# A gated-DeltaNet decoder layer: the token projections as blocks of 512 channels, with q, k, v and the attention queries transposed afterwards

## The chip, the core and the metric

The kernel runs on one core of one Trainium2 chip, in float32. The metric is the device time of one launch in microseconds, as the median of several runs. Everything happens in that one launch, with the inputs laid out beforehand by tiles in device memory.

## The reference, cut to what matters

One layer (DEPTH is 1) works on 256 tokens and 256 memory tokens of 2048 channels. Three things are multiplied onto each other at the end: a gated DeltaNet over 24 heads, a four-head cross-attention into the memory, and a SiLU gate over all 4096 inner channels.

```python
mem_n = rms_norm(mem, mem_norm_g)
h     = rms_norm(x, norm_g)
proj  = h @ dn_w_in                  # (256, 11312): q 1536 | k 1536 | v 3072 | a, b 48 | xq 1024 | z 4096
qkv   = silu(causal_depthwise_conv(proj[:, :6144], conv_w))      # 4 taps along the tokens
# per head: q, k l2-normed; g = -exp(a_log) * softplus(a + dt); beta = sigmoid(b)
o     = rms_norm(gated_delta_rule(q, k, v, g, beta), out_g)      # 24 heads of 128, state 128 x 128
xa    = softmax(rms_norm(xq) @ rms_norm(mem_n @ w_k).T / 16) @ (mem_n @ w_v)
y     = concat(o, xa) * silu(z)
out   = x + y @ w_out                # (256, 4096) @ (4096, 2048)
```

The convolution runs along the tokens for each channel by itself, which is why the kernel wants q, k and v with the channels on the partitions and the tokens along the row.

## The kernel before, in words

**Numbers.** Every large product is made exact by splitting each factor into a rounded part (`hi`, type float32r, made by a cast) and its remainder (`lo`, by a subtraction); three products hi·hi, hi·lo and lo·hi are summed in PSUM.

**The weight stream.** `PLAN` (line 51) lists 273 weight loads of 512 KB in the order in which TensorE wants them. `wraw` (line 271) issues a load on SyncE's queue into one of five raw buffers `st`; `wnext` (line 310) casts it on ScalarE to `hi` (line 326) and subtracts it on VectorE to `lo` (line 330), into one of four buffers `wt`; `wload` (line 335) keeps two loads ahead. Loads of kind Z fetch, for each partition, four pieces of 1 KB from four 128-channel weight tiles; all others are one piece of 4 KB per partition.

**Two forms of a projection.** `proj_a` (line 346) makes 128 channels at a time with channels on the partitions: the weights stand still and the tokens move. It takes 16 steps over the 2048 input channels, and each step is a pair of matmuls, one with 512 columns (hi and lo of the 256 tokens beside each other) and one with 256 (the weights' `lo` against the tokens' `hi`, added into the second half). The two halves of its bank are added afterwards in `halves` (line 375): a copy of 128x512 out of PSUM on ScalarE, an addition of 128x256 on VectorE. The 56 tiles of xq (8), k (12), q (12) and v (24) are made like this. `proj_b` (line 385) makes 512 channels at a time with tokens on the partitions, in two banks (r = 0 and 1, 128 tokens each); the tokens stand still and the weights move, with three matmuls of 512 columns per token half and step, 96 in all. The gate (z, `PLAN` kind "Z"), the memory's keys and values ("K", "V") and the output projection ("o") are made like this. In the first and the last load of a block, `proj_b` does all of r = 0 ahead of r = 1, so the r = 0 bank is done six matmuls before the block's end.

**What follows a projection.** A q, k or v tile goes through `conv` (line 813): one scaled copy on ScalarE, three multiply-adds on VectorE, one SiLU on ScalarE, all with the channels on the partitions. A k tile then feeds `gram` (line 846), whose results feed `inverse` (line 893: a loop of 31 small VectorE steps for six pairs of heads, twice) and `merge` (line 956: many small matmuls). `delta` (line 1108) runs the recurrence for one pair of heads: it begins when `Y` of the pair, its v tiles and the delta of the pair before are there. xq tiles go to `xq_done` (line 730) and `attend` (line 755); the latter takes the sum of squares of the query by four small matmuls into a bank of tag "tr" named `xss`. `split_y` (line 1057) transposes each finished 256-channel group of y (`pyT`) and splits it into hi and lo for the output projection, which takes the groups in the order 12 to 15 (attention), 0 to 11.

**PSUM.** The eight banks are dealt out by tag (line 168): `pa` 2, `m` 2, `tr` 1, `A` 2, `B` 1. Successive blocks of `proj_b` alternate between the two `A` and the two `pa` banks; `delta` also takes its banks `pU` and `pO` from `A`.

**The order of the work.** One Python loop (line 1269) writes out TensorE's projections in the order of `PLAN`. Everything else is a generator on a heap; after each group of matmuls `step_side` (line 214) lets those go on whose time has come by a modelled clock `now`, which adds a modelled cost per instruction (lines 122 to 133 and 198 to 208). `pe_soon` (line 228) postpones a process's next matmuls until its inputs should be there, plus 0.7 us; `calm` (line 240) keeps the VectorE's modelled queue under 1.6 us. The instructions of one engine run in the order in which they are queued. So a matmul whose input is late holds up every matmul behind it.

Of the kernel before, what the change touches and what calls it, by code (L numbers as in the profile page):

```python
# [44 lines left out]
LATE_DECAY = ("q", 3)  # L45
SPLIT = ("q", 9)
# [6 lines left out]


def _tiles(*ts):
    for t in ts:
        PLAN.extend([t, t])


for _t in range(8):  # L60
    _tiles(("x", _t))

for _t in range(6):
    _tiles(("k", _t))
    PLAN.extend([("Z", 6 + _t // 3)] * (3, 3, 2, 4, 4, 0)[_t])
for _t in range(3):
    PLAN.extend([("Z", _t)] * 8)
for _t in range(NPAIR):
    _tiles(("q", _t), ("v", 2 * _t), ("v", 2 * _t + 1))
    if _t < 2:  # L70
        _tiles(*[("k", _k) for _k in ((6, 7, 8), (9, 10, 11))[_t]])
    if _t in (1, 4, 7):
        PLAN.extend([("Z", 3 + _t // 3)] * 8)
# [4 lines left out]
STREAM = [_k for _k in PLAN if _k[0] != "Z"] + [("z", _t) for _t in range(32) for _ in range(2)]  # L78
N_PLAIN = len(PLAN) - 64
# [3 lines left out]
def hybrid_kernel(ctx: ExitStack, tc: tile.TileContext, x, xT, memT, W, prm_d, cst_d, out):  # L83
# [66 lines left out]
    s2p = ctx.enter_context(tc.tile_pool(name="s2p", bufs=60))  # L150
# [7 lines left out]
    def SM(name, shape, bufs=3, dt=F32):  # L158
        n = 1
        for d in shape:  # L160
            n *= d
        if n > 128:
            return smp.tile([128] + list(shape), dt, name=name, tag="s1k", bufs=10)
# [34 lines left out]
    def mm(o_, lhsT, rhs, start, stop):  # L198
# [3 lines left out]
        else:  # L202
            now[0] += max(0.092, n / 2400.0 + 0.017)
# [62 lines left out]
    wpos, plain, zpos = [0], [0], {}  # L266
# [4 lines left out]
    def wraw():  # L271
# [5 lines left out]
        if kind == "Z":  # L277

            s4 = zpos.get(t, 0)
            zpos[t] = s4 + 1  # L280
            u = N_PLAIN + 8 * t
# [3 lines left out]
        else:  # L285
            data = W[plain[0]]
# [23 lines left out]
    def wnext():  # L310
# [5 lines left out]
        if kind == "Z":  # L316
            hi, lo = [h.rearrange("p (k t c) -> p k t c", k=2, t=4) for h in (hi, lo)]
# [28 lines left out]
    def proj_a(done, tag="pa"):  # L346


        hold(lambda: spare(tag))
        pt = PS(tag, "pa")  # L350
        for kt in range(NKT):
            if kt % 8 == 0:
                wt = wload()
            hold(lambda: hs[kt] is not None)
            c = slice(kt % 8 * 128, (kt % 8 + 1) * 128)
            mm(pt, wt[:, 0, c], hs[kt].rearrange("p a t -> p (a t)"), start=(kt == 0), stop=False)
            mm(pt[:, 256:512], wt[:, 1, c], hs[kt][:, 0, :], start=False, stop=(kt == NKT - 1))
            if kt == NKT - 1:
                done(pt)
            yield kt % 8 == 7  # L360

# [23 lines left out]
    def proj_b(steps, act, tag, done, before=None):  # L385

        hold(lambda: spare(tag))
        pts = [PS(tag, "pb0"), None]
        n = len(steps)
        for s in range(0, n, 2):  # L390
# [8 lines left out]
            for i, (r, k2) in enumerate(rk):  # L399
                if pts[r] is None:  # L400
                    hold(lambda: spare(tag))
                    pts[r] = PS(tag, "pb1")
# [323 lines left out]

    xag = [None] * 4
    xq = [None] * 8

    def xq_done(t):  # L730
        def done(pt):
            hd, dt = t // 2, t % 2
            if dt == 0:
                xq[hd] = (S2("xqh", [2, 256], F32R), S2("xql", [2, 256], F32R), S2("xsq", [2, 256]))

            def go():
                yield 0.2
                qh, ql, sq = xq[hd]
                qf = yield from halves(pt)
                se.copy(qh[:, dt, :], qf)  # L740
                se.activation(sq[:, dt, :], qf, AF.Square)
                yield
                ve.tensor_tensor(out=ql[:, dt, :], in0=qf, in1=qh[:, dt, :], op=ALU.subtract)
                if dt == 1:
                    yield from attend(hd, qh, ql, sq)
# [9 lines left out]
    def attend(hd, qh, ql, sq):  # L755
        ve.tensor_tensor(out=sq[:, 0, :], in0=sq[:, 0, :], in1=sq[:, 1, :], op=ALU.add)
        yield from pe_soon()
# [10 lines left out]
        rq = SM("rq", [10], 2)  # L768
        ve.tensor_scalar(out=rq[:, 0:2], in0=pss[:, 0:2], scalar1=1.0 / 256, scalar2=EPS, op0=ALU.mult, op1=ALU.add)
        give(pss, ve.end)  # L770
        ve.tensor_reduce(out=rq[:, 4:6], in_=sc.rearrange("p (r m) -> p r m", r=2), axis=AX.X, op=ALU.max)
        yield
        rsqrt(rq[:, 2:4], rq[:, 0:2], 2)
# [39 lines left out]
    def conv(pt, ct, dst, name):  # L813
        acc = SM("acc", [256])
        w0 = P_CW + 4 * ct
        yield 0.2
        raw = yield from halves(pt)
        se.activation(acc, raw, AF.Copy, scale=prm[:, w0 + 3 : w0 + 4])
        yield
        for j in (1, 2, 3):  # L820
            ve.scalar_tensor_tensor(out=acc[:, j:256], in0=raw[:, 0 : 256 - j], scalar=prm[:, w0 + 3 - j : w0 + 4 - j],
                                    in1=acc[:, j:256], op0=ALU.mult, op1=ALU.add)
        yield
# [533 lines left out]
```

## Time and profile before

| | |
|---|---|
| median of 3 runs (lowest to highest) | 869.36 us (869.18 to 870.35) |
| the profiled execution's own time | 867.82 us |
| its span in the trace | 866.0 us |
| TensorE matmuls busy | 860.1 us (99%), 5092 instructions |
| TensorE weight loads busy | 729.3 us (84%) |
| VectorE busy | 638.8 us (74%) |
| ScalarE busy | 536.2 us (62%) |
| GpSimd busy | 39.5 us (5%) |
| DMA | 165.89 MB, mean 192 GB/s |

The span is the part of the execution that the trace covers; the execution's own time is 1.8 us longer, and the median of the timed runs is 1.5 us above that of the profiled execution. "PE" is the TensorE matmul, "PEld" its weight load, which overlaps the matmul before it; DVE is VectorE, ACT ScalarE, POOL GpSimd, SP SyncE. In the chain of waits the time is followed back from the last instruction to whatever released it. Its pieces have a start in us, a length in us, and what ran, with the number of instructions.

### The profile page before, as it was taken

To read this page: it belongs to the slowest core of one execution; us is meant where nothing else is said; L and a number is where in the kernel's file an instruction comes from. 1 tells how busy PE (TensorE), PEld (TensorE's weight loads), DVE (VectorE), ACT (ScalarE), POOL (GpSimd) and SP (SyncE) were. 2 spreads that over 40 slices of the span, in tenths; PEclk is the share of its full clock that TensorE was granted. 3 is DMA by queue.
4 is the path that set the end of the run, shared out by engine and by line. 5 is a ranking of instruction groups with operands and counts; after the bars stand their busy time and mean duration, and the time that the engine had idled before them with its cause. 6 is when DMAs were issued, how large, how long until landed. Compare 5 with 4: busy or idle time off the path is not lost.

```text
span 866.0 us, 13821 instructions
## 1 busy us (share of the span) xinstructions
PE 860.1 (99%) x5092; PEld 729.3 (84%) x5092; DVE 638.8 (74%) x1277; ACT 536.2 (62%) x904; POOL 39.5 (5%) x47
## 2 busy tenths in 40 slices
PE   9999999999999999999999999999999999999998
PEld 6888889888888888888888888878888888888886
DVE  7778898678786999588799898736888755454542
ACT  7655656678776665665578877756777654333331
POOL 1000000000010000001000010000000000000000
PEclk9999999999999999999999999999999999999999
DMA  9865554467878857555756546644344547766660
GB/s 353 312 208 183 171 173 145 135 200 223 266 223 232 256 195 189 193 167 185 209 191 201 190 146 205 182 138 146 122 147 146 170 155 231 235 205 206 204 199 25
DMA packets 97612, 165.89 MB, mean 192 GB/s; under 512 B 23280, under 2 KB 62984, under 8 KB 97544
## 3 DMA queue, kind: packets, MB, share of 16 engines
q1 hardware_dynamic: 97112, 164.72, 59.9%
q8 instruction: 40, 0.66, 0.3%
q10 hardware_dynamic: 432, 0.28, 0.1%
q14 instruction: 28, 0.23, 0.1%
HBM read 158.14 MB, written 6.84 MB: 191 GB/s over the span
## 4 chain that ended last, share of the span: by engine, by line
PE 99%; DMA 1%; DVE 0%; ACTq 0%; issue 0%; DVEq 0%
PE pb L96 51%; PE pa L96 37%; PE pO L96 2%; PE pm L96 2%; PE pkq L96 1%; PE pU L96 1%; PE pyT L96 1%; PE xsc L96 1%; PE xo L96 1%; PE pkk L96 1%; PE pvt L96 1%; DMA mst<-memT_d 1%; PE pqs L96 0%; PE pab L96 0%; PE xpT L96 0%; PE pk L96 0%
## 5 line engine op out<-in xcount | busy, mean ns | idle before, releaser
L330 DVE TENSOR_TENSOR wt<-st,wt 128x1024 fp32r<-128x1024 f32 (+1 forms) x274 | 333.5, 1218 | 143.8 <-ACT wt L326 140.1
L326 ACT CAST wt<-st 128x1024 fp32r<-128x1024 f32 (+1 forms) x274 | 286.3, 1047 | 173.1 <-PE pb L96 127.6
L96 PE MATMUL pa<-hkt,wt 128*128 128x512 f32 (+1 forms) x1792 | 334.6, 341 | 0.0
L96 PEld LDWEIGHTS pa<-hkt,wt 128*128 128x128 f32 x1792 | 274.3, 188 | 38.0 <-ACT zs L113 0.3
L96 PE MATMUL pb<-wt,hkt 128*128 128x512 f32 x768 | 182.2, 393 | 0.0
L96 PEld LDWEIGHTS pb<-wt,hkt 128*128 128x128 f32 x768 | 141.8, 188 | 28.9
L96 PE MATMUL pb<-wt,yhi 128*128 128x512 f32 x512 | 158.7, 391 | 0.0
L96 PEld LDWEIGHTS pb<-wt,yhi 128*128 128x128 f32 x512 | 95.3, 188 | 19.3
L96 PE MATMUL pb<-wt,ylo 128*128 128x512 f32 x256 | 99.7, 390 | 0.0
L96 PE MATMUL pb<-wt,mkt 128*128 128x512 f32 x384 | 91.3, 397 | 0.8 <-DVE mkt L113 0.5
L96 PEld LDWEIGHTS pb<-wt,mkt 128*128 128x128 f32 x384 | 72.7, 191 | 17.9 <-DVE wt L330 1.5
L113 DVE SCALAR_TENSOR_TENSOR acc<-raw,prm,acc 128x255 f32<-128x255 f32 x144 | 68.7, 478 | 6.9 <-ACT acc L113 5.8
L113 ACT COPY raw<-pa 128x512 f32<-128x512 f32 x56 | 32.8, 586 | 45.6 <-PE pa L96 45.5
L96 PEld LDWEIGHTS pb<-wt,ylo 128*128 128x128 f32 x256 | 48.1, 188 | 10.1
L113 ACT ACT_TABLE_LOAD x33 | 42.3, 1283 | 3.2 <-DVE acc L113 2.0
L113 DVE TENSOR_TENSOR raw<-raw 128x256 f32<-128x256 f32 x57 | 23.9, 419 | 14.6 <-ACT raw L113 14.3
L113 DVE TENSOR_TENSOR inT<-inXT,inN 96x1 f32<-96x1 f32 (+22 forms) x92 | 29.8, 342 | 1.0 <-PE pO L96 0.3
L113 DVE TENSOR_REDUCE inXT<-inT 96x1 f32<-96x1 f32 (+22 forms) x92 | 28.8, 337 | 0.6
L113 POOL TENSOR_TENSOR e<-e,mhalf 128x4 f32<-128x4 f32 x12 | 15.4, 1283 | 297.4 <-DVE e L113 277.0
L113 ACT ACTIVATE acc<-raw,prm 128x256 f32<-128x256 f32 x48 | 24.5, 510 | 4.9 <-DVE raw L113 4.9
L113 DVE TENSOR_SCALAR dec<-erow,gcc 128x128 f32<-128x128 f32 x96 | 23.8, 279 | 4.5 <-DMA erow<-dgc 4.5
L113 ACT ACTIVATE dec<-dec 128x512 f32<-128x512 f32 x24 | 15.2, 631 | 12.8 <-DVE dec L113 12.6
(197 smaller groups left out, 666.5 us busy)
## 6 DMA issues: line engine op xcount, KB each, us to landing
st<-W_d SPq DMA_DIRECT2D x272, 512.0 KB, 4.0
erow<-dgc SPq DMA_DIRECT2D x24, 256.0 KB, 4.8
dN<-dec SPq DMA_DIRECT2D x12, 256.0 KB, 3.6
xraw<-xT_d SPq DMA_DIRECT2D x8, 256.0 KB, 6.0
res<-x_d SPq DMA_DIRECT2D x8, 256.0 KB, 5.2
mst<-memT_d SPq DMA_DIRECT2D x7, 256.0 KB, 6.6
out_dram<-res SPq DMA_DIRECT2D x7, 256.0 KB, 5.0
inN<-dN SPq DMA_DIRECT2D x4, 192.0 KB, 4.3
```

Of the source, the lines that this page charges most:

```text
L96: return lambda *a, **k: pin(getattr(self.eng, op)(*a, **k))
L113: return pin(getattr(self.eng, op)(*a, **k))
L326: pin(se.eng.copy(hi[:, w] if parts > 1 else hi, st[:, w] if parts > 1 else src))
L330: pin(ve.eng.tensor_tensor(out=lo[:, w] if parts > 1 else lo, in0=st[:, w] if parts > 1 else src, in1=hi[:, w] if parts > 1 else hi, op=AL ...
```

## The change

All projections of tokens take the form of `proj_b`. The weights in memory stay in tiles of 128 channels; every load of x, k, q, v and z now gathers four pieces of 1 KB per partition, as the Z loads did. `proj_a`, `halves` for these tiles, `conv` and `xq_done` go. After a block of k, q or v, `tiles_done` copies the two banks to SBUF (two copies of 128x512 on ScalarE), transposes them on TensorE in two groups of four 128x128 pieces into a bank of tag "m" (two channel tiles per bank), and does the convolution of each tile with its input read from that bank. `x_done` does the same with one bank per head, and takes the sum of squares of the query on ScalarE while the tokens are on the partitions; the four small matmuls into `xss` go.

The order is now one of whole blocks: x0 k0 x1 k1 z6 z7 z0 z1 q0 v0 k2 v1 z2 q1 v2 z3 v3 q2 v4 z4 v5 z5, then the output projection. A block of k or q holds four pairs of heads' tiles, a block of v two pairs'. PSUM is dealt as `pa` 3, `m` 2, `tr` 1, `A` 1, `B` 1, and all token projections and the output projection rotate through the three `pa` banks. `delta` may begin when the delta two pairs before is done, and waits for the one before only ahead of its bank `A`. The second set of decays and `split_y` are started at other blocks.

```diff
-LATE_DECAY = ("q", 3)
-SPLIT = ("q", 9)
+LATE_DECAY = ("q", 1)
+SPLIT = ("z", 4)
...
+for _b in "x0 k0 x1 k1 z6 z7 z0 z1 q0 v0 k2 v1 z2 q1 v2 z3 v3 q2 v4 z4 v5 z5".split():
+    PLAN.extend([(_b[0], int(_b[1]))] * 8)
...
-    s2p = ctx.enter_context(tc.tile_pool(name="s2p", bufs=60))
+    s2p = ctx.enter_context(tc.tile_pool(name="s2p", bufs=59))
...
-    PB = {"pa": 2, "m": 2, "tr": 1, "A": 2, "B": 1}
+    PB = {"pa": 3, "m": 2, "tr": 1, "A": 1, "B": 1}
...
-            now[0] += max(0.092, n / 2400.0 + 0.017)
+            now[0] += max(0.092, n / 2400.0 + 0.0137) + 0.014 * (n == 256)
...
-        if kind == "Z":
+        if kind in TILES:
...
+    def x_done(b):
+        raw, rq = [None] * 2, [SM("rq", [10], 4) for _ in range(2)]
+        def done(r, pt):
+            def go():
+                yield 0.2
+                raw[r] = S2("raw", [512])
+                se.copy(raw[r], pt)
+                give(pt, se.end)
+                for hh in range(2):
+                    junk = SM("junk", [256])
+                    se.activation(junk, raw[r][:, hh * 256 : (hh + 1) * 256], AF.Square, accum_out=rq[hh][:, 8 + r : 9 + r])
+                if r == 0:
+                    return
+                yield from pe_soon()
+                for hh in range(2):
+                    hd = 2 * b + hh
+                    pk = yield from bank("m", "pxq")
+                    for dt in range(2):
+                        for r2 in range(2):
+                            tr(pk[:, dt * 256 + r2 * 128 : dt * 256 + (r2 + 1) * 128],
+                               raw[r2][:, hh * 256 + dt * 128 : hh * 256 + (dt + 1) * 128])
...
-        pss = yield from bank("tr", "xss")
-        for r in range(2):
-            mm(pss[:, r : r + 1], sq[:, 0, r * 128 : (r + 1) * 128], ones, start=True, stop=True)
...
+    def tiles_done(kind, b, taken):
+        raw = [None] * 2
+        def done(r, pt):
+            def go():
+                yield 0.2
+                raw[r] = S2("raw", [512])
+                se.copy(raw[r], pt)
+                give(pt, se.end)
+                if r == 0:
+                    return
+                yield from pe_soon()
+                for i in (0, 2):
+                    pk = yield from bank("m", "praw")
+                    for k in range(2):
+                        for r2 in range(2):
+                            tr(pk[:, k * 256 + r2 * 128 : k * 256 + (r2 + 1) * 128],
+                               raw[r2][:, (i + k) * 128 : (i + k + 1) * 128])
+                    yield 0.2
+                    accs = []
+                    for k in range(2):
+                        t = 4 * b + i + k
+                        src, acc = pk[:, k * 256 : (k + 1) * 256], SM("acc", [256])
+                        w0 = P_CW + 4 * (TAP[kind] + t)
+                        se.activation(acc, src, AF.Copy, scale=prm[:, w0 + 3 : w0 + 4])
+                        yield
+                        yield from calm()
+                        for j in (1, 2, 3):
+                            ve.scalar_tensor_tensor(out=acc[:, j:256], in0=src[:, 0 : 256 - j],
...
-                         and (p == 0 or f"d{p - 1}" in ready))
+                         and (p < 2 or f"d{p - 2}" in ready))
...
+        yield from until(lambda: p == 0 or f"d{p - 1}" in ready)
         A = yield from bank("A", "pU0")
...
-            return proj_b(order, y_act, "A" if t % 2 else "pa", out_done(t, res))
+            return proj_b(order, y_act, ("pa", "pa"), out_done(t, res))
...
-            return proj_b(kts, x_act, "pa" if t in (1, 3, 4, 5) else "A", z_done(t))
-        return proj_a({"x": xq_done, "k": k_tile_done, "q": q_done}[kind](t), "A" if kind == "x" and t < 2 else "pa")
+        return proj_b(kts, x_act, ("pa", "pa"), done)
```

More of the change, by code (lines that the diff above doesn't have):

```diff
@@ L343, in hybrid_kernel @@
     hs = [None] * NKT
[L346 to L360, printed above, removed]
     def proj_ab(done):
@@ L724, in decay @@
             dst[p] = d
+    TAP = {"q": 0, "k": 12, "v": 24}
     xag = [None] * 4
[L728 to L734, printed above, removed]
+    def x_done(b):
+        raw, rq = [None] * 2, [SM("rq", [10], 4) for _ in range(2)]
+        def done(r, pt):
             def go():
                 yield 0.2
[L738 to L745, printed above, removed]
+                raw[r] = S2("raw", [512])
[14 more added lines that the diff above has]
+                               raw[r2][:, hh * 256 + dt * 128 : hh * 256 + (dt + 1) * 128])
+                    yield 0.3
+                    qh, ql = S2("xqh", [2, 256], F32R), S2("xql", [2, 256], F32R)
+                    qhf, qlf = [t.rearrange("p a t -> p (a t)") for t in (qh, ql)]
+                    se.copy(qhf, pk)
+                    yield
+                    ve.tensor_tensor(out=qlf, in0=pk, in1=qhf, op=ALU.subtract)
+                    give(pk, ve.end)
+                    spawn(attend(hd, qh, ql, rq[hh]), max(ve.end - now[0], 0.0) + HOP)
+                    yield 2.0
             spawn(go())
@@ L810, in attend @@
         xag[hd] = xa
[L813 to L823, printed above, removed]
-        se.activation(dst, acc, AF.Silu)
-        yield from pe_soon()
-        ready.add(name)
+    def tiles_done(kind, b, taken):
[22 more added lines that the diff above has]
+                        se.activation(acc, src, AF.Copy, scale=prm[:, w0 + 3 : w0 + 4])
+                        yield
+                        yield from calm()
+                        for j in (1, 2, 3):
+                            ve.scalar_tensor_tensor(out=acc[:, j:256], in0=src[:, 0 : 256 - j],
+                                                    scalar=prm[:, w0 + 3 - j : w0 + 4 - j],
+                                                    in1=acc[:, j:256], op0=ALU.mult, op1=ALU.add)
+                        accs.append((t, acc))
+                    give(pk, ve.end)
+                    yield
+                    new = []
+                    for t, acc in accs:
+                        dst, name = taken(t)
+                        se.activation(dst, acc, AF.Silu)
+                        new.append(name)
+                    yield from pe_soon()
+                    ready.update(new)
+            spawn(go())
+        return done
@@ L1092, in hybrid_kernel, with q_tile, v_tile @@
     vps = [None] * NPAIR
[L1094 to L1106 removed]
+    def q_tile(p):
+        return KQ[p][:, 1, :], f"q{p}"
+    def v_tile(t):
+        p, i = divmod(t, 2)
+        if i == 0:
+            vps[p] = S2("vp", [2, 256])
+        else:
+            spawn(delta(p), 1.0)
+        return vps[p][:, i, :], f"v{t}"
     def delta(p):
[L1109 to L1110 removed]
+        yield from until(lambda: Y[p] is not None and dT[p] is not None and {f"q{p}", f"v{2 * p}", f"v{2 * p + 1}"} <= ready
+                         and (p < 2 or f"d{p - 2}" in ready))
         kq, vp, y, dt = KQ[p], vps[p], Y[p], dT[p]
```

100 lines of the change are left out of this document (37 added, 63 removed).

## The prediction

> **What bounds the kernel now.** I read the page's first lines, then the list of what TensorE waited for, then the chain of waits.
>
> ```profile
> span 866.0 us, 13821 instructions
> PE   860.1 (99%) x5092; PEld 729.3 (84%) x5092; DVE 638.8 (74%) x1277; ACT 536.2 (62%) x904; POOL 39.5 (5%) x47
> PEclk9999999999999999999999999999999999999999
> PE 99%; DMA 1%; DVE 0%; ACTq 0%; issue 0%; DVEq 0%
> ```
>
> The third line is the granted clock: full throughout. The fourth is the chain by engine: it stays on TensorE for 99% of the span. A matmul row's busy time also holds its latency, so "99% busy" alone would not prove that TensorE never waits. The list of waits does; its columns are total us, times, longest.
>
> ```profile
> PE warm L96 <- DVE warm L113: 1.2, 1, 1.2
> PE pb L96 <- DVE mkt L113: 0.5, 1, 0.5
> PE pb L96 <- DVE wt L330: 0.3, 1, 0.3
> ```
>
> That is the whole list for matmuls, 2.0 us, and the longest of them is the warm-up. So the time is the sum of TensorE's own work, in whatever order. Whatever the change takes off ScalarE, VectorE or the DMA queues gains nothing, and whatever it adds to TensorE is paid in full.
>
> **The change, term by term.** All terms are TensorE time, so I take the length of a step from pieces of the chain (start, length, instructions), not from an instruction's recorded duration.
>
> ```profile
> 253.92 55.09 PE pb L96 x243
> 309.01 31.08 PE pa L96 x176
> 475.97 8.87 PE pb L96 x39
> 485.29 8.18 PE pb L96 x36
> 505.73 7.97 PE pa L96 x46
> 514.14 10.41 PE pa L96 x60
> ```
>
> Removed: 56 tiles of the old form, that is 14 blocks of four tiles, each 4 x 16 = 64 pairs of a 512- and a 256-column matmul. A pair costs 31.08 / 88 = 0.3532 us in the quiet stretch at 309, but 7.97 / 23 = 0.3465 and 10.41 / 30 = 0.3470 in busy stretches. A block: 64 x 0.3470 = 22.21 to 64 x 0.3532 = 22.60.
>
> Added: 14 blocks of the new form, each 96 matmuls of 512 columns. One costs 55.09 / 243 = 0.2267 in the quiet, 8.87 / 39 = 0.2274 and 8.18 / 36 = 0.2272 between deltas. A block: 21.76 to 21.83. Both forms move the same columns, 64 x 768 = 96 x 512 = 49,152; the gain is only that 96 instructions have a smaller overhead than 128. It lies between 22.21 - 21.83 = 0.38 and 22.60 - 21.76 = 0.84 us a block. I take the middle, 0.61, because the pieces lie at both ends and the moved blocks run partly in the quiet (x, k) and partly between deltas (q, v): 14 x 0.61 = **-8.6 us**, bounds -5.3 and -11.8.
>
> Added: the transposes. Each of the 12 blocks of q, k, v has two groups of four, each of the two x blocks two groups (one per head): 28 groups. The same form stands in the trace as `pyT`, `pvt`:
>
> ```profile
> 610.86 0.44 PE pyT L96 x4
> 618.94 0.44 PE pyT L96 x4
> 646.19 0.44 PE pvt L96 x4
> 646.62 0.44 PE pyT L96 x4
> ```
>
> Every group is 0.44 us of the chain, alone between projections (610.86) or directly behind another group (646.62), so joining groups doesn't make them cheaper. 28 x 0.44 = **+12.3 us**, and I see no way below 28 x 0.40 = 11.2 or above 28 x 0.50 = 14.
>
> Removed: `xss`, four small matmuls for each of four heads.
>
> ```profile
> 149.59 0.34 PE xss L96 x4
> 149.93 1.54 PE xsc L96 x12
> 151.82 1.44 PE xo L96 x12
> ```
>
> They cost 0.34 themselves, and the twelve matmuls behind them take 1.54 where the twelve alike of `xo` take 1.44. Without `xss` I give `xsc` 1.44 too: 4 x (0.34 + 0.10) = **-1.8 us**, at the least -1.4.
>
> Sum: -8.6 + 12.3 - 1.8 = +1.9 us, with bounds -11.8 + 11.2 - 1.8 = -2.4 and -5.3 + 14 - 1.4 = +7.3.
>
> **What is costed at nothing, and its cover.**
>
> ```profile
> L113 ACT COPY raw<-pa 128x512 f32<-128x512 f32 x56 | 32.8, 586 | 45.6 <-PE pa L96 45.5
> L113 DVE TENSOR_TENSOR raw<-raw 128x256 f32<-128x256 f32 x57 | 23.9, 419 | 14.6 <-ACT raw L113 14.3
> L330 DVE TENSOR_TENSOR wt<-st,wt 128x1024 fp32r<-128x1024 f32 (+1 forms) x274 | 333.5, 1218 | 143.8 <-ACT wt L326 140.1
> L326 ACT CAST wt<-st 128x1024 fp32r<-128x1024 f32 (+1 forms) x274 | 286.3, 1047 | 173.1 <-PE pb L96 127.6
> L113 DVE SCALAR_TENSOR_TENSOR acc<-raw,prm,acc 128x255 f32<-128x255 f32 x144 | 68.7, 478 | 6.9 <-ACT acc L113 5.8
> 310.00:340.00 30.00, 30.00 (x172) 26.00 (x171) 29.07 (x55) 16.83 (x25) 0.00 (x0) 1.00 0.67 206
> ```
>
> ScalarE makes 28 bank copies in place of 56: 28 x 0.586 = 16.4 us less. VectorE loses 56 additions, 56 x 0.419 = 23.5 us. The last row is a stretch of 30 us with the busy time of PE, PEld, DVE, ACT and POOL, then clock, DMA share and GB/s: VectorE is busy for 29.07 us of 30, and TensorE doesn't wait even there, since the weights' subtraction (1.218 us) is needed once a load, which TensorE takes 12 x 0.227 = 2.7 us to use. So the relief is worth nothing, and the convolutions of four tiles arriving at once (12 multiply-adds, 12 x 0.478 = 5.7 us by the row of `acc`) are spread by `calm` inside a block of 21.8 us. If the cover fails, the next `wt` is late and TensorE pays it in full.
>
> ```profile
> st<-W_d SPq DMA_DIRECT2D x17, 512.0 KB, 4.9
> st<-W_d SPq DMA_DIRECT2D x10, 512.0 KB, 3.5
> ```
>
> DMA: 112 loads go from 4 KB to 1 KB pieces. The two `st` rows are the loads' median time to landing in the z stretch (255 to 305, 1 KB pieces) and in the stretch at 310 to 340 (4 KB): 4.9 against 3.5 us. Five raw buffers at 2.7 us a load leave 13 us, so 1.4 us more hides; the z stretch, at the 0.2267 quoted, shows that it does. SyncE's queue issues as many loads as before. Startup keeps its order and its four banks under other names: nothing.
>
> Banks: with three `pa`, the second half of a block needs the bank of the first half of the block before. That bank is done six matmuls before that block's end and is wanted six after it, 12 x 0.227 = 2.7 us later, for a copy of 0.59 us behind at most a cast of 1.05 us: nothing.
>
> **The rivals.**
>
> *New waits in TensorE's queue, above all at the tail (slower).* The new transposes wait for ScalarE's copy; queued behind them are the next block's matmuls, and everything waits for those. At the end, v now comes two pairs at a time, as v5 and z5 just ahead of the output projection.
>
> ```profile
> 645.32 0.87 PE pkq L96 x4
> 652.36 0.45 PE pU L96 x4
> 666.02 0.34 PE pqs L96 x4
> 667.90 0.87 PE pkq L96 x4
> 679.58 2.74 PE pb L96 x12
> 694.22 0.87 PE pkq L96 x4
> 724.30 0.44 PE pyT L96 x4
> 724.75 137.42 PE pb L96 x606
> ```
>
> A delta begins with `pkq` and ends with `pqs`; the begins lie 22.6 and 26.3 us apart, and the last pair's `pyT` comes 30 us after its `pkq`, 44.7 us into the output projection (start 679.58), just in time. After the change pairs 6 to 11 wait for the second inverse to be loaded and merged, which waits until pair 5's delta has read `Y` for the last time.
>
> ```profile
> 347.50 0.93 PE pm L96 x65
> 365.71 0.84 PE pm L96 x24
> 662.68 0.81 PE pO L96 x7
> ```
>
> A merge runs from 347.50 to 366.55, 19 us; a delta's last read of `Y` is the piece at 662.68, 17 us after its `pkq`. With a block at 21.8 us and T from one delta's begin to the next: pair 4 begins some 6 us after v2 (copy, transposes, convolution: an estimate from 0.59 + 0.44 + 4 x 0.478 and their queues), pair 5 T later, pair 6 another 17 + 6 (the load) + 19 later; that is T + 48 after v2, T + 4 after v3. Pair 11 follows after 5 T and its `pyT` after 30 more: 6 T + 34 from v3's end. The output projection's last load of its first block comes at 5 x 21.8 + 41 = 150. At the old T of 22 that is 166, 16 us late, and all of it TensorE's: 871.3 + 16 = 887; at 21 it is 10 late, 881; from 19.3 down nothing is. Against it: the change lets a delta's first part (645.32 to 652.36, 7 us) run ahead of the one before, which brings T towards 666.02 - 652.36 = 14 us.
>
> *The matmul term is larger (not slower).* If the old form's blocks are all worth the quiet 22.60 and the new ones 21.76, the gain is 11.8 and the sum -1.3 us: 868.1. It decides from 0.75 us a block on, where 14 x 0.75 = 10.5 pays 12.3 - 1.8. For it: half the old pieces have 0.353. Against: q and v, 36 of the 56 tiles, lie where the pieces have 0.347.
>
> *Transposes cost their recorded duration.*
>
> ```profile
> L96 PE MATMUL pyT<-cst,o 128*128 128x128 f32 x48 | 7.2, 273 | 0.0
> ```
>
> If they did not overlap, 112 x 0.273 = 30.6 us in place of 12.3: 871.3 + 18.3 = 889.6. Against it stand the 0.44 us for four. The Trainium skill ("TensorE: Matmul & The Clock Gate", Part 4, PE-mode transpose) gives about 275 ns for one in a kernel's context, and says that the full clock doesn't engage for transposes; by that the change would lose those 18 us more. The trace agrees on the duration (273 ns) but not on the price in a stream (0.11 us each), and the clock row is full where `pyT` runs.
>
> *The change relieves something that I don't see* (fewer breaks among the small matmuls of `merge`, another cut of the groups): 2 to 4 us less than the sum, 867.
>
> **How the numbers follow.** The profiled execution took 867.82 us, 1.8 over its span, and the median of the runs is 869.36, 1.54 above it. Sum against the profiled run: 867.82 + 1.9 = 869.7; for the median, +1.54: **871.3 us**. About 0.2%, 1.7 us, is what a measurement of this kernel can tell from no change: 867.6 to 871.1 is the same.
>
> Chances: the sum without new waits 0.53 (its own range 869.5 to 873.5); new waits 0.22 (881 and up to 887); the larger matmul term 0.16 (868.1); the full price of transposes 0.01 (889.6); an unseen relief 0.08 (867). The first is split by the boundary at 871.1: about 0.36 slower, 0.17 the same. The third is same for 0.12 and faster for 0.04; the last is faster. Slower 0.36 + 0.22 + 0.01 = 0.59; same 0.17 + 0.12 = 0.29; faster 0.04 + 0.08 = 0.12. The range reaches from where a tenth is left below, 867.5, to where a tenth is left above, 882.
>
> **What would show it.** In the profile after: pieces of the new `pb` at 0.227 a matmul between the first memory blocks and the output projection; 28 groups of `praw` and `pxq` at 0.44; no `xss`, and `xsc` at 1.44; a list of waits for PE of about 2 us. Right would be a chain still 99% on TensorE. Wrong would be PE waits on ACT `raw` or on `yhi`, `ylo` in the output projection (the waits rival), a block of the new form under 21.7 us, or a group above 0.5 us.

## The result, and the profile after

The changed kernel takes **873.16 us** (median of 8 runs, 872.10 to 875.98) where the kernel before takes 868.93 us on the same chip (867.05 to 870.35, 8 runs). The ratio is 1.0056, 95% interval 1.0041 to 1.0071: about 4.2 us slower, and the interval lies wholly above 1. The prediction was 871.3 us, slower with a chance of 0.59.

The page of the changed kernel begins like this; the last two lines are the clock row and the chain by engine.

```profile
span 870.9 us, 13037 instructions
PE 863.8 (99%) x4740; PEld 715.6 (82%) x4740; DVE 618.9 (71%) x1213; ACT 507.8 (58%) x866; POOL 37.2 (4%) x47
PEclk9999999999999999999999999999999999999999
PE 67%; DVE 0%; DVEq 0%; issue 0%
```

TensorE is still 99% busy, with 352 instructions fewer and 3.7 us more. VectorE has lost 20 us and ScalarE 28 us, and the kernel is slower: the relief bought nothing. The chain shows 67% because it can be followed back only to 280.22 us. There a weight load of TensorE stood 0.5 us for ScalarE's SiLU out of a bank of z (`zs`), and the next matmul came 0.2 us late. From there on the chain stays on TensorE, but for its very end. The waits of TensorE (total us, times, longest) in the changed kernel:

```profile
PE warm L83 <- DVE warm L100: 1.2, 1, 1.2
PE pb L83 <- DVE mkt L100: 0.9, 1, 0.9
PE pb L83 <- DVE wt L319: 0.3, 1, 0.3
PE xpT L83 <- DVE dec L100: 0.2, 1, 0.2
```

That is 2.6 us in all, against 2.0 before: no new wait to speak of. The first three stand in the first 7 us. The groups that correspond to those quoted of before:

```profile
L83 PE MATMUL pb<-wt,hkt 128*128 128x512 f32 x2112 | 511.3, 395 | 0.1
L319 DVE TENSOR_TENSOR wt<-st,wt 128x1024 fp32r<-128x1024 f32 (+1 forms) x274 | 333.3, 1217 | 177.6 <-ACT wt L315 175.5
L100 DVE SCALAR_TENSOR_TENSOR acc<-praw,prm,acc 128x255 f32<-128x255 f32 x144 | 68.6, 477 | 7.1 <-ACT acc L100 5.6
L100 ACT COPY raw<-pb 128x512 f32<-128x512 f32 x28 | 16.3, 583 | 8.6 <-PE pb L83 8.3
```

The weight loads (number, size, median us to landing) and the stretch from 310 to 340 us (busy PE, PEld, DVE, ACT, POOL, then clock, DMA share, GB/s):

```profile
st<-W_d SPq DMA_DIRECT2D x272, 512.0 KB, 4.2
```

```profile
310.00:340.00 30.00, 30.00 (x138) 24.86 (x137) 27.43 (x54) 15.72 (x20) 0.00 (x0) 1.00 0.66 201
```

The 56 additions are gone, the copies are 28 at 583 ns, a load lands 4.2 us after its issue over the whole kernel, and VectorE still works 27.43 us of 30 in a stretch through which TensorE runs without a gap. In the chain of waits (start, length, instructions) the new work is seen where it was forecast, at the forecast length:

```profile
325.44 0.44 PE praw L83 x4
325.88 4.34 PE pb L83 x19
...
465.25 0.44 PE praw L83 x4
465.69 10.91 PE pb L83 x48
476.60 0.44 PE praw L83 x4
```

For the balance I added up, from the trace's instruction records, the intervals from the start of each TensorE matmul to the start of the next, by the bank written (an interval includes a wait, if there is one). "Without transposes" is the first experiment below; us:

```
                                        before    after   without transposes
memory projections and warm-up           94.72    96.02     95.62
token projections (pa, and pb on hkt)   498.85   493.62    491.19
praw and pxq (the 28 groups)              0       10.39      0
xss and xsc                               7.52     5.88      5.72
pm (merge)                               13.11    12.43     13.37
all the rest                            246.35   246.68    246.39
sum                                     860.55   865.02    852.29
```

The first row is work that the change doesn't touch, so a difference in it is not the change's; one experiment below tests that. Without it the changed kernel's TensorE needs 769.00 - 765.83 = 3.2 us more.

### The profile page after: what moved, and what is told of

It reads as the page before. It is cut to its first block, busy times and chain, and to the rows that moved or that the text cites. A ratio compares the mean times of both kernels' runs of the same rounds, so it can differ in the third digit from the quotient of the medians.

```text
span 870.9 us, 13037 instructions
## 1 busy us (share of the span) xinstructions
PE 863.8 (99%) x4740; PEld 715.6 (82%) x4740; DVE 618.9 (71%) x1213; ACT 507.8 (58%) x866; POOL 37.2 (4%) x47
## 4 chain that ended last, share of the span: by engine, by line
PE 67%; DVE 0%; DVEq 0%; issue 0%
PE pb L83 58%; PE pO L83 2%; PE pm L83 1%; PE pkq L83 1%; PE pU L83 1%; PE praw L83 1%; PE pyT L83 1%; PE pvt L83 1%; PE pqs L83 0%; PE pkk L83 0%; DVE res L100 0%; DVEq L1362 0%
## 5 line engine op out<-in xcount | busy, mean ns | idle before, releaser
L83 PE MATMUL pb<-wt,hkt 128*128 128x512 f32 x2112 | 511.3, 395 | 0.1
L83 PEld LDWEIGHTS pb<-wt,hkt 128*128 128x128 f32 x2112 | 387.8, 188 | 77.2 <-ACT zs L100 0.5
L100 DVE SCALAR_TENSOR_TENSOR acc<-praw,prm,acc 128x255 f32<-128x255 f32 x144 | 68.6, 477 | 7.1 <-ACT acc L100 5.6
L83 PEld LDWEIGHTS pb<-wt,ylo 128*128 128x128 f32 x256 | 48.1, 188 | 10.2
L100 ACT ACTIVATE acc<-praw,prm 128x256 f32<-128x256 f32 x48 | 22.6, 471 | 14.9 <-PE praw L83 8.0
L100 POOL TENSOR_TENSOR e<-e,mhalf 128x4 f32<-128x4 f32 x12 | 13.0, 1083 | 283.4 <-DVE e L100 283.4
L100 DVE SCALAR_TENSOR_TENSOR o<-o,e,zs 128x128 f32<-128x128 f32 x48 | 14.9, 346 | 11.2 <-POOL e L100 11.2
L100 ACT COPY raw<-pb 128x512 f32<-128x512 f32 x28 | 16.3, 583 | 8.6 <-PE pb L83 8.3
L100 POOL TENSOR_TENSOR srk<-skt,mhalf 128x2 f32<-128x2 f32 x12 | 10.5, 879 | 223.9 <-DVE skt L100 223.9
L100 ACT ACTIVATE ojunk<-o 128x128 f32<-128x128 f32 x48 | 14.5, 303 | 7.5 <-DVE o L100 6.3
```

What stands on the lines that cost most here:

```text
L83: return lambda *a, **k: pin(getattr(self.eng, op)(*a, **k))
L100: return pin(getattr(self.eng, op)(*a, **k))
```

## The experiments

Each edit is against the changed kernel, where nothing else is said. Ratios are to the kernel before, run on the same chip.

**The transposes left out.** The groups and their bank go; what follows reads the token-major copy in SBUF as if it were transposed.

```diff
-                    pk = yield from bank("m", "praw")
-                    for k in range(2):
-                        for r2 in range(2):
-                            tr(pk[:, k * 256 + r2 * 128 : k * 256 + (r2 + 1) * 128],
-                               raw[r2][:, (i + k) * 128 : (i + k + 1) * 128])
+                    pk = raw[i // 2]
...
-                    pk = yield from bank("m", "pxq")
...
+                    pk = raw[hh]
```

> The changed kernel with its 28 groups of four transposes left out: the convolutions and the split of the attention queries read the copied banks as they are, so what is computed from q, k, v and xq is not the reference's. Theory 1 (the sum of TensorE's work as predicted, 0.44 us a group): 12.3 us less than the changed kernel, 873.2 - 12.3 = 860.9, that is 8 us under the kernel before, a ratio of 0.990 to 0.991. What is left between this and the kernel before is then the matmul term and the four xss groups, 8.6 + 1.8 = 10.4 less about 1.3 for a slower start. Theory 2 (a break in the new form's stream costs more than the group: the matmuls behind a group run slower for a while): 0.49 to 0.50 a group, 13.7 to 14 us, so 859.3, ratio 0.989, and the stream's own mean per matmul falls. Theory 3 (new waits behind the copies matter): more than 14 us.

Measured: 860.18 us, ratio 0.9897 (0.9878 to 0.9916), between theory 1 (860.9) and theory 2 (859.3). The transposes are 873.16 - 860.18 = 13.0 us of the change by the medians, 865.02 - 852.29 = 12.7 by all of TensorE's intervals, and 769.00 - 756.67 = 12.3 without the first row of the table. That is 0.44 to 0.46 us a group. Without them the change gains 9.1 us by the medians (869.30 here before). Its chain has the longest undisturbed piece of the new form:

```profile
257.63 87.73 PE pb L83 x387
```

87.73 / 387 = 0.2267 us a matmul, 21.76 a block: the bottom of the forecast's range for a block, to the last digit. The same run also gives the matmul term by itself: 491.19 - 498.85 = -7.7 us, where -8.6 was forecast. Over all 2112 matmuls of the new form, those behind small matmuls included, the mean interval there is 491.19 / 2112 = 0.2326 us.

**Each group of transposes done twice.**

```diff
+                    for _ in range(2):
                         for k in range(2):
                             for r2 in range(2):
                                 tr(pk[:, ...], raw[r2][:, ...])
```

(the same for `pxq`)

> The changed kernel with every group of four transposes issued twice, the second four directly behind the first into the same bank. Theory 1: the second four cost 0.44 like the first, +12.3 us, 885.5, ratio 1.019 to the kernel before. Theory 2: the same, since the number of breaks stays: +12.3. If a transpose cost its recorded 0.273 us: +30.6 us, 904. If transposes directly behind others were cheaper than 0.11 each, less than 12.

Measured: 885.65 us, ratio 1.0186 (1.0169 to 1.0204), 12.5 us above the changed kernel, as theory 1 had it (885.5). By the intervals `praw` and `pxq` go from 10.39 to 22.59 us, 12.2 more, 0.436 for the second four of a group. (The profiled execution, 887.4 us, has two further waits of 1.0 and 1.2 us, at 306 and 359 us.) The chain, the clock row and the instruction's own row in this kernel (last: shortest, median and longest duration in ns):

```profile
329.44 0.87 PE praw L83 x8
```

```profile
PEclk9999999999999999999999999999999999999999
```

```profile
L83 PE MATMUL praw<-cst,raw x192: 270/272/328, 156.5 to 686.6; 128*128 128x128 f32 x192
```

Eight transposes take 0.87 us of the chain, 0.11 each, though each has a recorded duration of 0.272. So the rival that priced them by their duration (30.6 us) is refuted from both sides, by leaving out and by doubling: 13.0 and 12.5. The Trainium skill ("TensorE: Matmul & The Clock Gate", Part 4, PE-mode transpose) says about 275 ns for one and that the full clock doesn't engage for them. The trace agrees with the duration, as a latency. It shows no slower clock for them: the clock row is in its top tenth in every slice, and 128 columns of an ordinary float32 matmul in the changed kernel (`pkq`) take 0.108 to 0.110 us to the next start, as a transpose does (0.109). Whether a long stretch of transposes alone would get the full clock, no run here shows.

**One transpose at a time.** After each transpose of a `praw` group some projection matmuls are put in, so that a group of four makes four breaks in the stream instead of one.

```diff
                         for r2 in range(2):
+                            if k or r2:
+                                yield 0.6
                             tr(pk[:, ...], raw[r2][:, ...])
```

> The changed kernel with the four transposes of each praw group issued one by one, three projection matmuls between them: 24 groups become 96, nothing else is added. Theory 1 (a transpose costs 0.11 us wherever it stands): 873.2, no difference. Theory 2 (the matmuls behind a break run slower for a while; the first three of them lose about 0.025 us together by the trace of the changed kernel): 72 x 0.025 = +1.8 us, 875.0, and the mean of a projection matmul rises from 0.2283. If a break itself, whatever its length, costs a switch of about 0.08: +6 us, 879.

Measured: 875.05 us, ratio 1.0073 (1.0056 to 1.0091); the changed kernel again, on the same chip (next experiment), has 873.85 and 1.0053, so the two intervals overlap. The median alone would also fit theory 2 (875.0); what decides is the trace. In the chain:

```profile
325.52 0.11 PE praw L83
325.63 0.69 PE pb L83 x3
326.32 0.11 PE praw L83
326.43 0.69 PE pb L83 x3
```

By the intervals, `praw` and the token projections together take 499.33 + 2.90 = 502.23 us, against 493.62 + 8.91 = 502.53 in the changed kernel. 72 more breaks cost nothing there. How that comes about is seen in single starts, of the changed kernel and of this one (start in us, bank, interval to the next start):

```
changed kernel          one at a time
325.045 pb    0.235     325.124 pb    0.233
325.280 praw  0.109     325.357 praw  0.027
325.389 praw  0.108     325.384 pb    0.313
325.497 praw  0.109     325.697 pb    0.229
325.606 praw  0.029
325.635 pb    0.316
325.951 pb    0.235
```

The matmul behind a transpose starts 0.03 us after it, and then takes 0.087 us longer than the usual 0.227: what looks like a penalty on the projection is the rest of the transpose's own 0.11. A group costs 3 x 0.109 + 0.029 + (0.316 - 0.227) = 0.445, and a single transpose 0.027 + (0.313 - 0.227) = 0.113. The three matmuls behind that are a few thousandths above 0.227 on the mean (0.230, 0.233 and 0.234), which would make 0.46 of the group. The doubling gave 0.436, so between 0.44 and 0.46 these runs don't decide. It doesn't matter whether transposes stand together. (Elsewhere, in the small matmuls of `merge` and the deltas, this run takes some 2 us more than the first profile of the changed kernel; that cause stays open.)

**Both kernels once more.** No edit.

> The kernel before once more, for the first 40 us of its trace. Theory 1: the start differs from run to run by about 1 us with the arrival of the first loads, so this profile shows another start than the first one, and the 1.3 us that the changed kernel lost there in its profile are not the change's. Rival: the start of the kernel before is the same again within 0.3 us, and the slower start belongs to the change.

> The changed kernel once more, for the same: theory 1 has its start vary by about 1 us between this and the first profile; the rival has it at the same place within 0.3 us, 1.3 us behind the kernel before. The sum over TensorE behind the start should be the same within 0.5 us.

Measured: before 869.16 us, ratio 1.0003 (0.9993 to 1.0013); after 873.85, ratio 1.0053 (1.0034 to 1.0071). The profiled execution of before has a span of 868.3 us this time, where the one on which the prediction stands has 866.0. By the intervals 2.23 of the 2.3 us lie in the first stage: the memory projections and the warm-up take 96.95 where they took 94.72; everything behind it takes 765.85 and took 765.83. Its waits:

```profile
PE pb L96 <- DVE mkt L113: 1.1, 2, 0.8
```

So the first stage moves by 2 us from execution to execution of one and the same kernel. The wait for the memory tokens (0.5 in the first profile) is the smaller part of it. The larger part is speed: the 512-column matmuls of the memory start 0.427 us apart until 10.2 us in the first profile and until 13.7 us in the second, and 0.227 apart from there on. In 3.4 us that is 8 matmuls with 0.2 us more each, 1.6 us. In the two profiles of after the faster spacing comes for good at 12.4 and 11.7 us, and the stage takes 96.02 and 95.45. So theory 1 holds for the start. The rest takes 769.00 and 770.16 us in these two, further apart than the 0.5 that was expected: `merge` takes 12.43 and 13.87, since the second profile has a wait there that the first doesn't have:

```profile
PE pm L83 <- issue: 1.3, 1, 1.3
```

**The deltas one after the other.** `delta` may begin only when the pair before is done, as in the kernel before.

```diff
-                         and (p < 2 or f"d{p - 2}" in ready))
+                         and (p == 0 or f"d{p - 1}" in ready))
```

> The changed kernel with one condition put back: a delta waits at its begin for the one before, not for the one two before. My arithmetic in the rival: the period of the deltas goes back to 21 to 26 us, and the last pair's transposes come 10 to 16 us late for the output projection, 883 to 889 with TensorE waiting there. The rival view: the arithmetic overstates what the second inverse delays, the last pair is still in time, and the time stays within 1 us of 873.2.

Measured: 878.44 us, ratio 1.0102 (1.0084 to 1.0119): 5.3 us more than the changed kernel. It is neither the rival's 883 to 889 nor within 1 us of 873.2, and it doesn't come for the reason that the tail rival gave. Its waits and a stretch of its chain:

```profile
PE pm L83 <- issue: 2.7, 1, 2.7
PE pb L83 <- DVE wt L319: 1.1, 2, 0.6
PE pU L83 <- DVE ul L100: 0.5, 1, 0.5
```

```profile
564.57 1.06 PE pm L83 x76
565.62 2.70 issue
568.32 1.22 PE pm L83 x52
569.54 3.01 PE pb L83 x8
...
733.89 137.43 PE pb L83 x606
```

The last `pyT` starts at 733.62, 44.6 us into the output projection (start 689.03), and there is no wait of the output projection for `yhi` or `ylo`: the piece from 733.89 on is one run of 606 matmuls up to 871.32, in a span of 875.6. Of TensorE's 4.7 us more in the profile, 3.6 lie in `pm` (16.00 against 12.43), inside the second merge. 2.7 of them are the wait. Behind it TensorE runs slower for a while: the granted clock is 0.57 of full speed between 568 and 572 us, and the eight projection matmuls from 569.54 take 3.01 us, where eight at 0.227 take 1.8. What "issue" stands for, and why this order brings that wait, the profile doesn't show and no run tried: the cause of the wait stays open.

In the changed kernel the tail has more room than before: the last `pyT` starts at 723.51, 37.9 us into the output projection (685.64), where it started 45.1 us into it before. Lines of its chain's end:

```profile
712.86 0.44 PE pO L83 x4
713.30 0.34 PE pqs L83 x4
713.64 9.70 PE pb L83 x42
723.34 0.44 PE pyT L83 x4
723.78 142.86 PE pb L83 x630
```

**v without transposes.** If some 0.45 us a group is what the change loses, the 12 groups of v and the 12 `pvt` (which turn v back into token order) could both go: v's convolution can run with tokens on the partitions, if rows shifted by one to three tokens are read back from device memory and each tap's weights are a row of 512 channels. VectorE then does seven operations of 128x512 for each half of the tokens, in place of twelve multiply-adds for a block's four tiles.

```diff
+                sy.dma_start(dv[b][3 + 128 * r : 131 + 128 * r, :], raw[r])
...
+                w3, _ = load(3)
+                nxt = load(2)
...
+                for r2 in range(2):
+                    yield from calm()
+                    ve.tensor_tensor(out=acc[r2], in0=raw[r2], in1=w3, op=ALU.mult)
+                for j in (2, 1, 0):
+                    w, sh = nxt
+                    if j:
+                        nxt = load(j - 1)
+                    yield 1.0
+                    for r2 in range(2):
+                        yield from calm()
+                        ve.tensor_tensor(out=sh[r2], in0=sh[r2], in1=w, op=ALU.mult)
+                        yield from calm()
+                        ve.tensor_tensor(out=acc[r2], in0=acc[r2], in1=sh[r2], op=ALU.add)
...
-                w = (2 * b + h) * C
-                se.activation(vs[:, b, h, :], vt[:, w : w + C], AF.Copy, scale=...)
+                se.activation(vs[:, b, h, :], vp[b][:, cv + h * C : cv + (h + 1) * C], AF.Copy, scale=...)
```

> The changed kernel, with the convolution of v done while the tokens are on the partitions: each copied bank of v goes to device memory, comes back three times shifted by one to three tokens, and VectorE multiplies it with the taps, which are loaded as rows spread over the partitions. The 12 groups of praw for v and the 12 groups of pvt in the deltas go; the same result is computed. VectorE gets about 14 x 0.686 us in place of 12 x 0.478 us a block of v, 6 x 3.9 = 23 us, and DMA some 15 MB more. If TensorE's sum is all that counts: -12 x 0.455 - 12 x 0.44 = -10.7 us against the changed kernel, 862.5, ratio 0.992 to the kernel before. If the load that is put on VectorE, SyncE's queue and DMA no longer hides: weights come late, TensorE waits for wt, and the time is above 866.

Measured: 868.62 us (12 runs, 866.28 to 871.82), ratio 0.9994 (0.9982 to 1.0006): 4.5 us better than the changed kernel (5.2 against its 873.85 on the same chip), and no better than the kernel before. The intervals of `praw` and `pvt` do go down by 4.73 + 4.51 = 9.2 us, but 3.2 come back in the token projections, 1.0 in the output projection, and 2.3 in the first stage, which varies anyway. The new waits, and the stretch from 500 to 530 us (busy PE, PEld, DVE, ACT, POOL, then clock, DMA share, GB/s):

```profile
PE pb L83 <- DVE wt L319: 3.5, 4, 1.5
PE pU L83 <- DVE eq L100: 0.7, 1, 0.7
PE pyT L83 <- DVE ylo L100: 0.7, 1, 0.7
```

```profile
500.00:530.00 30.00, 27.34 (x122) 21.76 (x121) 29.45 (x63) 16.74 (x26) 0.00 (x0) 1.00 0.65 210
```

Of the 3.5 us, 0.8 stand in the first stage (at 6.6 and 10.5 us), and 2.7 at 507 and 510 us. VectorE is nearly full there and TensorE isn't any more: 27.34 us of 30. VectorE's work is now late for TensorE, either because there is too much of it or because it stands 4.9 us for the loads of the shifted rows; the last two runs below were made to tell these apart.

**The multiplications on GpSimd.** In v_tokens, the multiplications of taps 0 to 2 are issued on GpSimd, which is nearly idle (5%), and the additions come later by the planned clock; the second run also has the blocks in the order v4, v5, z4, z5 and `SPLIT` at v5, the third is the second with 4.5 us in place of 3.0 ahead of the additions.

```diff
                     for r2 in range(2):
-                        yield from calm()
-                        ve.tensor_tensor(out=sh[r2], in0=sh[r2], in1=w, op=ALU.mult)
+                        po.tensor_tensor(out=sh[r2], in0=sh[r2], in1=w, op=ALU.mult)
+                    yield 3.0
+                    for r2 in range(2):
                         yield from calm()
                         ve.tensor_tensor(out=acc[r2], in0=acc[r2], in1=sh[r2], op=ALU.add)
```

> The kernel with v's convolution in token order, with six of its eight multiplications a block moved from VectorE to GpSimd, and 3 us more between them and the additions. In the last run of that kernel TensorE waited 3.5 us for wt around 517 us, where VectorE was busy 29.45 of 30 us and stood 4.9 us for the shifted rows. If VectorE is the cause, those waits go: 868.6 less 4 to 6 us, 863 to 865. If GpSimd and VectorE slow each other, or the last pairs come too late for the output projection, the time stays at 868 or rises.

> The same with v5 ahead of z4 and the splitting of y started at v5: the last two pairs begin one block earlier. If lateness at the output projection is what holds the one before, this gains on it, 861 to 864; if only VectorE does, it is the same within 1 us.

> The same again with 4.5 us in place of 3 between GpSimd's multiplications and VectorE's additions. If VectorE still stands in its queue for GpSimd's products, weights behind it are late and the longer pause helps, 1 to 2 us under the one before; if not, the same within 1 us.

Measured: 899.26 us (ratio 1.0349, 1.0331 to 1.0367), 900.78 (1.0357, 1.0338 to 1.0377) and 890.33 (1.0245, 1.0225 to 1.0265): all far slower. In the first of them:

```profile
L100 POOL TENSOR_TENSOR sh<-sh,wv x36: 1262/1305/2387, 361.3 to 693.6; 128x512 f32<-128x512 f32 x36
L100 DVE TENSOR_TENSOR vt<-vt,sh x36: 676/682/1781, 363.6 to 699.8; 128x512 f32<-128x512 f32 x36
```

```profile
PE pb L83 <- ACT zs L100: 4.2, 1, 4.2
PE pU L83 <- DVE o L100: 4.2, 1, 4.2
PE pqs L83 <- DVE eq L100: 3.2, 1, 3.2
PE pyT L83 <- DVE kcl L100: 3.0, 1, 3.0
```

A multiplication of 128x512 takes at the median 1.3 us on GpSimd, up to 2.4; and the additions on VectorE, which all took 0.68 to 0.69 us in v_tokens, now take up to 1.78. The additions stand for GpSimd (15.5 us in all), and what is queued behind them on VectorE stands too: the deltas and, through them, TensorE. TensorE loses twice: in the first of these runs the trace's clock record falls to half in three stretches (432.5 to 439.4, 521.3 to 528.1 and 569.1 to 572.5 us), and each of its three longest waits ends in or just ahead of one. With the additions 1.5 us later (the third run against the second) the kernel takes 10 us less, where 1 to 2 were expected. That is in line with this, but the split between the waits, the slower operations and the half clock wasn't measured.

**Later multiplications, and v ahead.** In v_tokens VectorE stood 4.9 us for the shifted rows' loads, so the multiplications were put off by 1.5 us more of planned stream; the second run adds the order v4, v5, z4, z5.

```diff
-                    yield 1.0
+                    yield 2.5
```

> v's convolution in token order as in the run before with it (v_tokens, 868.6 us, 4.6 below the changed kernel where 10.7 were forecast), and one number changed: the multiplications of a tap come 2.5 us of planned stream after the loads of its shifted rows are issued, where they came 1.0 after. In v_tokens VectorE stood 4.9 us for those loads, and TensorE stood 3.5 us for VectorE's weight parts. Theory 1 (the late loads are what makes VectorE late): TensorE's wait for the weight parts goes from 3.5 us to under 1, time 865 to 866. Theory 2 (VectorE simply has too much work between the deltas, 29.45 of 30 us busy): the wait stays at 2.5 or more, time 868 to 869.

> The same as v_later, with the blocks in the order v4, v5, z4, z5 in place of v4, z4, v5, z5 (and the second inverse's solve started one block later in the list, at v5): v's last convolution and the last deltas have two z blocks before the output projection. If theory 1 holds, the order adds nothing, since no wait at the tail was seen: 865 to 866 as v_later. If VectorE's load between the deltas is the limit, two v blocks back to back make it worse there: 869 to 872. If an unseen wait at the end of the deltas costs something, 862 to 864.

Measured: 873.06 us (1.0046, 1.0031 to 1.0061) and 875.95 (1.0065, 1.0048 to 1.0083). Theory 1 fell: in the first of them, v_later, TensorE's wait for the weights is not below 1 us but larger than in v_tokens (3.1 against 2.7 without the first stage), and VectorE stands longer for the same loads, not shorter.

```profile
PE pb L83 <- DVE wt L319: 4.3, 5, 1.4
PE pO L83 <- DVE vs L100: 1.6, 1, 1.6
PE pO L83 <- ACT o L100: 1.4, 1, 1.4
```

```profile
DVE sh L100 <- DMA sh<-dv: 11.3, 6, 3.2
```

```profile
500.00:530.00 30.00, 26.15 (x116) 20.27 (x115) 26.83 (x63) 11.79 (x14) 0.00 (x0) 1.00 0.58 179
```

The waits of TensorE come first, then the one of VectorE, then the stretch from 500 to 530 us. Theory 2 has the wait for the weights right (2.5 or more), but not the time, which it put at 868 to 869, nor its reason: VectorE is less full in that stretch than in v_tokens (26.83 against 29.45), and TensorE stands more. What makes VectorE late in these kernels is thus not settled by the two. A tap's loads are issued ahead of the tap before it, so putting off the multiplications puts off the loads as well; what moves the loads alone was not tried. The order v4, v5 cost 2.9 us more, so v's convolution at the end was not what held the kernel up; the profiled execution of that run is 4 us under its median, so its trace doesn't show where.

No version beats the kernel before.

## Why the prediction was right, and where it was off

**The direction held, the size didn't.** The sum gave +1.9 us and the medians give +4.2, more than twice as much. The time itself is 1.9 us above the forecast and not 2.3, since the kernel before was 0.4 us faster in this comparison (868.93) than in the one on which the sum was built (869.36). The forecast of 871.3 lay 0.2 us above the prediction's own limit of 871.1 for "the same". That the result is clearly slower has something of luck in it: the errors in the terms were small, but none of them went the other way.

**The bound was read rightly.** Everything that TensorE does is paid in full, and the rest isn't. The 20 us taken off VectorE and 28 off ScalarE bought nothing: TensorE's intervals grow by 865.02 - 860.55 = 4.5 us and the span by 4.9. One reading was off, in the first stage, which the change leaves alone: TensorE isn't at full speed throughout. In the trace of before, matmuls of 512 columns start 0.427 us apart until 10.2 us, which neither the clock row nor the list of waits shows. v_tokens shows the limit of the bound: "the relief is worth nothing" held for taking VectorE's work away, not for adding to it. There TensorE waits 2.7 us for the weights' subtraction around 508 us.

**The matmul term: -8.6 forecast, -7.7 measured.** Mechanism and bounds (-5.3 to -11.8) held; the middle value that I took, 0.61 us a block, was too large (14 times that is 8.54, which I rounded up). It is 7.66 / 14 = 0.55. The long pieces gave the new form rightly (0.2267 in the quiet), but only a few blocks are quiet. The larger-gain rival (-11.8) is refuted by the same number.

**The transposes: +12.3 forecast, +12.2 to +13.0 measured.** The price of 0.44 us a group was right within what these runs can tell (0.44 to 0.46), and it is the rate in the stream that was paid and not the recorded duration.

**xss: -1.8 forecast, -1.6 measured** (7.52 to 5.88; 5.72 in the run without transposes).

With the measured terms the sum is -7.7 + 12.8 - 1.6 = +3.5, where 12.8 is praw and pxq with all that the projections' intervals differ by (10.39 + 493.62 - 491.19). That 12.8 is an upper figure: 0.8 of it are three places, at 191, 201 and 280 us, where the matmul behind a projection matmul comes late. The run without transposes doesn't have them. The intervals outside the first stage give +3.2 and, from the second pair of profiles, +4.3, where the wait of 1.3 us in `merge` is in it. The medians give 4.2. The remaining 0.7 us I can't place: it is no larger than what the first stage and `merge` vary by.

**The base.** The sum was made against a profiled execution and 1.54 us were added to reach the median. That was sound: the second profile of before, 2.3 us longer, has all its excess in the first stage.

**What was costed at nothing.** Casts, subtractions, copies, smaller DMA pieces, the banks: after the first stage the list of waits after has nothing for the weights, for `raw` or for a bank. Three weight loads stand all the same, two for VectorE's decays (`dec`, at 191 and 201 us) and one for the SiLU out of a bank of z (at 280): these are the 0.8 us above. The convolutions of four tiles at once are hidden.

**The tail rival (881 to 887) did not come, and its arithmetic was wrong on both sides.** It took 21.8 us a block from v3's end to the output projection: 5 x 21.8 = 109. Those blocks also carry the small matmuls of merge, deltas and gates, and took 149.2 us (536.4 to 685.64), 30 each. So the deltas had 40 us more than I gave them. But they also came later than its 6 T + 34, which is 166 us behind v3's end for T = 22: the last `pyT` starts 187 us behind it in the changed kernel (723.51 - 536.4), and 198 with the deltas in series (733.62 - 535.9), where the last six pairs begin 22 to 25 us apart. Even that, which was the rival's own condition, didn't make the output projection wait; the 5.3 us which it cost arose elsewhere. How much later the last delta could come without a wait, no run shows.

**Unseen relief** (867) did not show.

## What to carry to other kernels

Where one engine is busy throughout and its list of waits is empty, an exchange of instructions is settled by their spacing in its stream: here 128 matmuls became 96 for 0.55 us a block, and the two groups of transposes that such a block needs cost about 0.9. A recorded duration is a latency and no price; the start of the next instruction is, and leaving the work out or doubling it confirms it in one run each. Where the terms nearly cancel, as here, small errors in each decide the sum: say how far apart they lie before calling its sign. When a deadline is worked out, take the length of a stage from the stage as it runs, with all that is interleaved in it, and not from its purest stretch.

## What the runs showed of the hardware that I had not expected

A transpose's cost falls on the instruction behind it: the projection matmul starts 0.03 us after a transpose, and then takes 0.31 us to the next start in place of 0.227, so that the sum is the same however the transposes are spread (502.23 and 502.53 us).

A 512-column matmul behind a 256-column one takes longer than among its own kind: in the kernel before, at 309 to 340 us, its intervals are 0.232 to 0.241 us (mean 0.236), against 0.227 in the new form. Those of the 256-column ones are 0.113 to 0.120 (mean 0.117), against half of 0.227, 0.1135. So the loss of the old form lies in both of its matmuls, more of it in the long one.

The first stage (memory projections and warm-up, 94.7 to 97.0 us) varies by 2 us from one execution to the next in the same kernel, half of the difference that was to be measured. It follows the time from which on 512-column matmuls start 0.227 us apart and no longer 0.427: 10.2 us in the first profile of before (94.72 for the stage), 12.4 in after (96.02), 13.7 in the second of before (96.95), 15.3 in v_tokens (98.35).

Long waits of TensorE were followed, or ended, by a stretch at half clock: 3.4 us of it at the 2.7 us wait of the serial deltas (568.2 to 571.6 us), and 17 us in all at the three waits of 3.2 to 4.2 us in the first GpSimd run. Two further waits in that run, of 3.0 and 2.8 us, had none.

A float32 matmul of 128 columns (`pkq`, 0.108 to 0.110 us) is spaced like a transpose (0.109), and one of 384 columns takes 0.321 to 0.325, while a projection matmul on float32r takes 0.227 for 512: per column that is about half as much.

GpSimd's multiplication of 128x512 takes 1.26 to 2.39 us where VectorE's takes 0.69, and VectorE's additions in that kernel reach 1.78 us.
